# A diffusion block with S5, latent attention and experts: the prologue put in another order

## The chip, the cores and the metric

The kernel runs on one core of a Trainium2 chip. The metric is the device time of one execution in microseconds (us). The engines are TensorE (PE, with its weight loads as PEld), VectorE (DVE), ScalarE (ACT), GpSimd (POOL) and SyncE (SP), which here issues nearly all transfers. Each engine works through its own queue in order.

## The reference, cut to what matters

One layer works on 512 latent tokens and 256 context tokens of width 1024, in float32:

```python
mod_x = silu(c) @ w_ada + b_ada
hx = modulate(rmsnorm(x, norm1_g), sh1x, sc1x)
ux, qax, kvax, krx, gatex = split(hx @ w_in)
lam_bar, b_bar = s5_discretise(lam_re, lam_im, log_dt, b_re, b_im)
xs_x = s5_scan(s5_drive(ux, b_bar), lam_bar, rev, h0)
x_mid = x + g1x * merge_branches(ssm_x, attn_x, gatex, w_out)
x = x_mid + g2x * expert_choice_ffn(hx2, ...)
```

`hc` and `uc` are the same for the context. The change is in the first part: the adaLN shift and scale, the modulated tokens, the input projection and the S5 branch (32 groups of 16 channels, both directions). Attention and the 16 experts follow and are not touched.

## The kernel before, in words

The prologue, up to the end of the input projection, is scheduled by hand: inside `tc.manual_schedule()` every engine runs its instructions in the order in which the program issues them. Buffers come from pools with a fixed count, and an instruction that takes a buffer waits until the former user is done.

The work is this. `pk`, one packed load of small parameters, and the tokens `X` (L215 to L219) are loaded, then the S5 parameters `craw` and `braw` (L220 to L223), then the adaLN weights in four parts (`wada_load`, L227), the last part only after the first half of the tokens has been transposed, since it takes one of their buffers. ScalarE squares the tokens, VectorE normalises them (`xnorm`), TensorE transposes them (`xt_half`, L343) into `xt` for latent and `hc` for context tokens. `rr` deals out the instructions of several generators in turn, which sets VectorE's order; `late_by` delays one of them. Among them are the S5 parameters: `powers` and `powers2` (powers of the discretised eigenvalues: `lt_`, `lq`), `rot` (L429, the rotations `e8`) and `bbar_g` (L453).

The adaLN product (`ada_part`, L188) has eight k-steps of four 32-row matmuls. `ada_end` (L192) copies it to SBUF on ScalarE and turns it into columns `acol`, which give the scale and shift `ab1`. With them the tokens are modulated for each of eight k-tiles: a high part on ScalarE (L636) and a low part on VectorE, two operations (L108 and L93). `mm3` (L120) multiplies in three matmuls: high by high, high by low, low by high.

The input projection has 25 blocks of 128 columns: four `u` (for S5), three `q`, two `kv`, sixteen gate blocks `g`. `win_load` loads a block's weights, `win_prep` (L608) splits them on ScalarE and VectorE into `ws`, a pool of two buffers. `win_block` (L650) does 24 matmuls into a buffer of the pool `psg` (two buffers, by `pg`). `u` and `kv` blocks have a context part too (`ctx_block`, L658), 8 matmuls into another buffer of that pool. `f_kv` (L690) reads its latent product by ScalarE and, for the low part of the result, by VectorE (`stt`).

S5 works in four rounds `gb`. Their parameters come from `s5_P` and `s5_R` on POOL (L507, L571; R needs `e8`), and from `s5_Q` on VectorE (L521), which `s5_B` transposes on TensorE (L531). `s5_K` (L547) makes a kernel of short lags. A round itself is `s5_V` (L755: the drive on TensorE, then multiplications by R, a scan and multiplications again on VectorE), `s5_Y` (L789: output matmuls, which need the scan's result `Xc`), `s5_T` and `s5_out`. Blocks of `fill` (all but the `u` blocks, in the order of `order`) are put between by `fill_one` (L833), so that TensorE has work while VectorE scans: two after each `s5_V`, one after `s5_Y`, one after `s5_out`. The five left over run in a tail, each with one split of weights for the next stage; constants on VectorE (L930 to L970 or so) stand before the tail.

Before the change, block `u` 0 is multiplied alone as tokens are modulated; the other `u` blocks follow, with the parameters of round 0 and 1 between them, and then the rounds.

Of the kernel before, what the change touches and what calls it, by code (L numbers as in the profile page):

```python
# [8 lines left out]
F32 = mybir.dt.float32  # L9
# [46 lines left out]
def hybrid_block(ctx: ExitStack, tc: tile.TileContext, A, out, dbg=None, stop=99):  # L56
# [12 lines left out]
    cur = {}  # L69

    def cst(name, shape, dt=F32, p="const"):
        return (const if p == "const" else cur[p]).tile(shape, dt, name=name, tag=name)

    def tl(p, name, shape, dt=F32):
        return cur[p].tile(shape, dt, name=name, tag=p)
# [139 lines left out]
    for j in range(4):  # L215
# [1 line left out]
        dma(t[0:NCX], cv[:, 2 * j:2 * j + 2, :])  # L217
        dma(t[NCX:NCH], xv[:, 2 * j:2 * j + 2, :])
        X.append(t)  # L219
    craw = cst("craw", [128, 2, 32, 16], p="early")  # L220
    dma(craw, A["ssm_c"])
    braw = tl("qq", "braw", [128, 2, 32, 16])
    dma(braw, A["ssm_b"])  # L223
    hc = tl("hxp", "hc", [128, 8, 256])
    wt = {}

    def wada_load(kh, tags):  # L227
        q = 0
        while q < 4:
            n, big = tags.pop(0)  # L230
            t = tl(n, f"wada{kh}{q}", [128, 2, 2, 512] if big else [128, 1, 2, 512])
            for i in range(1 + big):
                wt[kh, q] = t[:, i]
                dma(t[:, i], wada_src(0, 2, kh, q))
                q += 1

    wada_load(0, [("hxp", 1), ("hxp", 1)])
    wada_load(1, [("hxp", 1), ("hxp", 1)])
    wada_load(2, [("m4", 0), ("m4", 0), ("rr", 0), ("rr", 0)])

    S.activation(sc2v[:, 0], P("c"), AF.Silu)
    S.activation(sc2v[:, 1], P("cc"), AF.Silu)
# [88 lines left out]
    def xnorm(hf):  # L331
        l0 = 4 * hf
        vx = sm("vx", [NCH, 4])
        ts(vx, ssx[:, l0:l0 + 4], 1.0 / D, EPS)
        yield
        yield from rsqrt_g(rstd[:, l0:l0 + 4], vx, [NCH, 4])
        for l in range(l0, l0 + 4):
            ts(X[l // 2][:, l % 2, :], X[l // 2][:, l % 2, :], rstd[:, l:l + 1])
            yield
# [143 lines left out]
    rr(expm1_parts(za, ex, em1), trig(), late_by(5, xnorm(0)))  # L483
    S.activation(sh, br, AF.Sin)
    S.activation(ch, ab, AF.Sin)
    rr(xnorm(1), late_by(2, powers2()), late_by(2, powers()), late_by(8, xt_half(0)))
    wada_load(3, [("zz", 0), ("xc", 0), ("xx", 1)])
    pada = pg("ada0")
    for k in range(2):
        ada_part(pada, k, [wt[0, q][:, k] for q in range(4)])  # L490
    rr(xt_half(1), rot(), late_by(8, bbar_g()))
    for k in range(2, 8):
        ada_part(pada, k, [wt[k // 2, q][:, k % 2] for q in range(4)])

    PTs, RTs, MTs, BTs, Qs = {}, {}, {}, {}, {}
    SH = [128, 8, 8, 16]
# [87 lines left out]

    bd = tl("bd", "bd", [128, 2, 8, 32])
    G.memset(bd, 0.0)
    s5_P(0)
    s5_R(0)
    pha.close()
    for n, k in (("uf", 1), ("sq", 3), ("gt", 3), ("kr", 1), ("ws", 2), ("raw", 4)):  # L590
        cur[n] = pool(n, ph1, bufs=k)
    order = [(f, b) for f, bs in (("u", range(4)), ("g", (0, 1)), ("kv", (0,)), ("g", (2, 3, 4)), ("kv", (1,)),
                                  ("g", (5, 6, 7)), ("q", (0, 1)), ("g", (8, 9)), ("q", (2,)), ("g", range(10, 16)))
             for b in bs]
    base = {"u": 0, "q": 512, "kv": 896, "g": 1184}
    wins, preps = [], {}
    nxt = {"load": 0, "prep": 0}

    def win_load():
        if nxt["load"] < len(order):  # L600
            f, b = order[nxt["load"]]
            nxt["load"] += 1
            w = tl("raw", f"win_{f}{b}", [128, 8, 128])
            c = base[f] + 128 * b
            dma(w, win[:, :, c:c + 128])
            wins.append(w)

    def win_prep():  # L608

        if nxt["prep"] < len(order):  # L610
            fb = order[nxt["prep"]]
            nxt["prep"] += 1
            raw = wins.pop(0)
            ws = tl("ws", "ws", [128, 2, 8, 128], F32R)
            S.activation(ws[:, 0], raw, AF.Copy)
            preps[fb] = ws, raw
            if fb == ("u", 0):
                return
            sub(ws[:, 1], raw, ws[:, 0].bitcast(F32))
            if fb[0] not in ("u", "kv"):  # L620
                win_load()

    for _ in range(4):
        win_load()
    wkr = tl("kr", "wkr", [128, 8, 32])
    dma(wkr, win[:, :, 1152:1184])
    ada_end(0, pada, tl("dt", "adar0", [128, 512]), win_prep)
    ab1 = cst("ab1", [128, 2, 8, 2])
    c0 = acol[:, 0].rearrange("p (u q) b s -> p u (q b) s", u=2)
    V.tensor_copy(ab1[:, 1], c0[:, 0])  # L630
    stt(ab1[:, 0], c0[:, 1], 1.0, P("g1n")[:, :, None].to_broadcast([128, 8, 2]), ALU.add, ALU.mult)
    hx = [[tl("hxp", f"hx{i}{j}", [128, 4, 512], F32R) for j in range(2)] for i in range(2)]
    for k in range(8):
        x = xt[k // 4][:, k % 4, :]
        hi, lo = [hx[i][k // 4][:, k % 4, :] for i in range(2)]
        S.activation(hi, x, AF.Identity, scale=ab1[:, 0, k, 0:1], bias=ab1[:, 1, k, 0:1])  # L636
        S.activation(hc[:, k, :], hc[:, k, :], AF.Identity, scale=ab1[:, 0, k, 1:2], bias=ab1[:, 1, k, 1:2])
        h = tl("gt", "hxf", [128, 512])
        ts(h, x, ab1[:, 0, k, 0:1], ab1[:, 1, k, 0:1])
        sub(lo, h, hi.bitcast(F32))  # L640
        if k == 0:
            ws, raw = preps["u", 0]
            sub(ws[:, 1], raw, ws[:, 0].bitcast(F32))

    def hxs(k, tok=slice(0, 512)):
        return [hx[i][k // 4][:, k % 4, tok] for i in range(2)]

    def win_block(f, b):  # L650

# [3 lines left out]
            mm3(p, [ws[:, i, k, :] for i in range(2)], hxs(k), k == 0, k == 7)  # L655
        return p, raw

    def ctx_block(raw):  # L658
        p = pg("pc", (128, 256))
        for k in range(8):  # L660
            T.matmul(p, raw[:, k, :], hc[:, k, :], start=(k == 0), stop=(k == 7))
        return p
# [175 lines left out]
            later.remove(x)  # L838
            sumsq(*x)

    win_prep()
    s5_Q(0)
    o = f_u(0)
    win_prep()
    u_out(0, *o)
    us_ = {0: s5_U(0)}
    o = f_u(1)
    win_prep()
    u_out(1, *o)
    s5_B(0)  # L850
    o = f_u(2)
    s5_bd(0)
    win_prep()
    u_out(2, *o)
    s5_K(0)
    s5_P(1)
    s5_R(1)
    o = f_u(3)
    win_prep()
    u_out(3, *o)  # L860
    for gb in range(4):
        U, rt = us_.pop(gb)
        Xc = s5_V(gb, U, rt)
        fill_one()
        fill_one()
        win_prep()
        win_prep()
        if gb < 3:
            s5_Q(gb + 1)
        yb = s5_Y(gb, U, Xc)  # L870
        if gb < 3:
            us_[gb + 1] = s5_U(gb + 1)
            s5_bd(gb + 1)
        if gb < 2:
            s5_P(gb + 2)
            s5_R(gb + 2)
        fill_one()
        t, y = s5_T(gb, yb)
        run_late()
        s5_out(gb, t, y)  # L880
        win_prep()
        if gb == 1:
            f_kr()
        fill_one()
        if gb < 3:
            s5_K(gb + 1)
            s5_B(gb + 1)
            win_prep()
# [81 lines left out]
    bh = cst("bh", [128, 4])  # L970
    ts(bh, P("bglu"), 0.5)

    tail = [(), (t_wkv,), (t_wg,), (t_ysp, 0), (t_ysp, 1)]
    while fill:
        win_prep()
        fill_one()
# [660 lines left out]
```

## Time and profile before

| | us |
|---|---|
| median of 3 runs (lowest to highest) | 1933.91 (1933.46 to 1936.47) |
| profiled execution, its own time | 1933.22 |
| its span | 1931.4 |
| TensorE busy in the span | 1661.3 (86%) |
| VectorE busy | 530.1 (27%) |
| ScalarE busy | 320.6 (17%) |
| POOL busy | 209.7 (11%) |
| mean rate of HBM, read and written, over the span | 332 GB/s |

The busy shares are means over stages with different limits. The prologue takes the first 310 us, attention and the router the next 290, the experts the rest. In a timeline line the columns are start, duration, engine, line, operation, output<-inputs, sizes and count, and in brackets the idle time before it and what ended that. The granted clock is 1.00 at TensorE's full 2.4 GHz and 0.50 at 1.2 GHz.

### The profile page before, as it was taken

The page shows a single profiled execution, that of the slowest core. Times are in us where ns is not written, and L with a number is a line of the kernel's source. Part 1 is how long each engine was busy: PE and PEld are TensorE (multiplying, and loading weights), DVE is VectorE, ACT ScalarE, POOL GpSimd, SP SyncE. Part 2 cuts the span into 40 slices and gives each one's busy share as a digit, 9 for nine tenths or more (in the row PEclk, how much of TensorE's full clock was granted, in tenths as well). Part 3 has the DMA queues.
Part 4 walks back from the last instruction along what each step waited for, and adds up shares of the span by engine and source line. Part 5 has one row for each costly group of instructions (what it writes and reads, how often), then busy time and mean ns, then how long its engine had stood idle before and what let it go on. Part 6 is the DMA issues. An engine that isn't in the chain of part 4 may idle for free.

```text
span 1931.4 us, 21472 instructions
## 1 busy us (share of the span) xinstructions
PE 1661.3 (86%) x8660; PEld 806.7 (42%) x8660; DVE 530.1 (27%) x1180; ACT 320.6 (17%) x593; POOL 209.7 (11%) x218
## 2 busy tenths in 40 slices
PE   4798999999996998888888888888888888888887
PEld 2576778755673343323333233333323233332322
DVE  8877655666744100000010010101000010000000
ACT  3422225464421100000000000000000000000000
POOL 3767100231110000000000000000000000000000
PEclk8899999999997999999999999999999999999999
DMA  9253353434675999999999999999999999999997
GB/s 315 64 144 110 109 190 112 169 125 176 170 290 223 419 414 420 414 414 419 414 414 419 414 420 415 419 414 414 420 415 420 414 419 414 414 420 414 420 414 286
DMA packets 149122, 642.61 MB, mean 333 GB/s; under 512 B 14752, under 2 KB 49568, under 8 KB 84128
## 3 DMA queue, kind: packets, MB, share of 16 engines
q1 hardware_dynamic: 145504, 631.81, 82.1%
q0 software_dynamic: 2880, 7.34, 1.7%
q10 hardware_dynamic: 640, 2.10, 0.4%
q8 instruction: 68, 1.11, 0.2%
q14 instruction: 30, 0.25, 0.0%
HBM read 623.93 MB, written 17.27 MB: 332 GB/s over the span
## 4 chain that ended last, share of the span: by engine, by line
PE 45%; DMA 34%; DVE 7%; issue 5%; ACT 3%; POOL 2%; POOLq 0%; SPq 0%; ACTq 0%; DVEq 0%
DMA wu<-in_w_e_up 16%; PE pgu L1504 15%; DMA wg<-in_w_e_gate 9%; DMA wd<-in_w_e_down 8%; PE pdn L1519 8%; PE pxg L1457 2%; PE po L1259 1%; DVE hd L93 1%; PE px L121 1%; PE px L123 1%; PE px L122 1%; ACT hd L1506 1%; PE ada L190 1%; PE phT L1511 1%; PE py L800 1%
## 5 line engine op out<-in xcount | busy, mean ns | idle before, releaser
L1504 PE MATMUL pgu<-wu,xe 128*64 128x512 f32 (+1 forms) x1536 | 630.1, 562 | 31.8 <-DMA wu<-in_w_e_up 31.7
L1504 PE MATMUL pgu<-wg,xe 128*64 128x512 f32 (+1 forms) x1536 | 635.7, 562 | 1.2 <-DVE xe L93 1.2
L1519 PE MATMUL pdn<-wd,hT 128*64 128x512 f32 x1408 | 365.5, 650 | 32.1 <-ACT hT L1513 32.1
L93 DVE TENSOR_TENSOR hd<-hd,pgu 64x512 f32<-64x512 f32 x96 | 62.0, 645 | 1011.4 <-ACT hd L1506 1011.4
L1504 PEld LDWEIGHTS pgu<-wg,xe 128*64 128x64 f32 x1536 | 207.3, 138 | 258.6 <-issue 240.8
L1504 PEld LDWEIGHTS pgu<-wu,xe 128*64 128x64 f32 x1536 | 207.8, 138 | 179.5 <-issue 124.1
L1506 ACT ACTIVATE hd<-pgu 64x512 f32<-64x512 f32 x96 | 53.2, 555 | 967.7 <-PE pgu L1504 967.7
L1519 PEld LDWEIGHTS pdn<-wd,hT 128*64 128x64 f32 x1408 | 114.3, 147 | 215.6 <-issue 164.6
L1538 POOL DMA_INDIRECT out<-ye,sidx x16 | 24.9, 1555 | 1354.9 <-DVE ye L111 1208.4
L1511 PE MATMUL phT<-pk,hd 64*128 64x64 f32 x352 | 42.0, 236 | 118.3 <-DVE hd L93 118.2
L1511 PEld LDWEIGHTS phT<-pk,hd 64*128 64x128 f32 x352 | 28.9, 138 | 195.9 <-DVE hd L93 195.9
L121 PE MATMUL px<-hx,ws 128*128 128x512 f32 x200 | 82.5, 413 | 6.1 <-ACT hx L636 6.1
L122 PE MATMUL px<-hx,ws 128*128 128x512 f32 x200 | 81.0, 405 | 3.3 <-DVE hx L93 3.3
L123 PE MATMUL px<-hx,ws 128*128 128x512 f32 x200 | 80.6, 403 | 1.4 <-DVE ws L93 1.4
L1457 PE MATMUL pxg<-xm,oh 128*64 128x512 f32 x256 | 75.5, 620 | 0.6 <-DVE oh L93 0.6
L1513 ACT COPY hT<-phT 128x256 f32<-128x256 f32 x96 | 34.0, 354 | 119.7 <-PE phT L1511 119.7
L121 PEld LDWEIGHTS px<-hx,ws 128*128 128x128 f32 x200 | 39.1, 195 | 15.3 <-ACT hx L636 6.2
L122 PEld LDWEIGHTS px<-hx,ws 128*128 128x128 f32 x200 | 38.9, 194 | 14.8 <-DVE hx L93 7.5
L123 PEld LDWEIGHTS px<-hx,ws 128*128 128x128 f32 x200 | 38.8, 194 | 10.5 <-DVE ws L93 2.5
L1461 DVE COPY xg<-pxg 128x256 f32<-128x256 f32 x16 | 6.8, 424 | 128.6 <-ACT xg L1460 128.6
L1457 PEld LDWEIGHTS pxg<-xm,oh 128*64 128x64 f32 x256 | 30.1, 142 | 22.9 <-issue 21.3
L1229 DVE TENSOR_REDUCE mx<-ps 128x1 f32<-128x768 f32 x32 | 30.5, 954 | 27.7 <-PE ps L123 25.0
(473 smaller groups left out, 1767.2 us busy)
## 6 DMA issues: line engine op xcount, KB each, us to landing
wg<-in_w_e_gate SPq DMA_DIRECT2D x176, 1024.0 KB, 19.9
wu<-in_w_e_up SPq DMA_DIRECT2D x164, 1024.0 KB, 19.9
wd<-in_w_e_down SPq DMA_DIRECT2D x163, 1024.0 KB, 19.9
wada<-in_w_ada SPq DMA_DIRECT2D x16, 1024.0 KB, 7.3
wd<-in_w_e_down SPq DMA_DIRECT2D x26, 512.0 KB, 18.7
wu<-in_w_e_up SPq DMA_DIRECT2D x24, 512.0 KB, 18.0
wada<-in_w_ada SPq DMA_DIRECT2D x16, 512.0 KB, 10.6
win_g<-in_w_in SPq DMA_DIRECT2D x16, 512.0 KB, 4.2
```

The lines of the kernel that those rows point to most:

```text
L93: (e or V).tensor_tensor(o, a, b, op=op)
L121: T.matmul(o, a[0], b[0], start=first, stop=False)
L122: T.matmul(o, a[0], b[1], start=False, stop=False)
L123: T.matmul(o, a[1], b[0], start=False, stop=last)
L1229: V.tensor_reduce(mx, p[:, 0:768], AX.X, ALU.max, negate=True)
L1457: T.matmul(px[64 * h:64 * h + 64, :], oh[:, t], xms[t][:, 512 * h:512 * h + 512], start=(t == 0), stop=(t == 3))
L1504: T.matmul(p[64 * j:64 * j + 64, :fn], xe[:, k, :], wt_[8 * j + k], start=(k == 0), stop=(k == 7))
L1506: S.activation(hd[:, :fn], p[0:64, :fn], AF.Silu)
L1511: T.transpose(ph[:, b, :], hd[:, 128 * b:128 * b + 128], ident[0:64, 0:64])
L1513: S.copy(hT[:, :n], ph[:, :n])
L1519: T.matmul(po[64 * h:64 * h + 64, :], hT[:, b, :], w[:, 512 * h:512 * h + 512], start=(f0 == 0 and b == 0), stop=(f0 + 128 * b == FF - 128))
L1538: G.indirect_dma_start(out=o2, out_offset=bass.IndirectOffsetOnAxis(ap=sidx, axis=0), in_=ye, in_offset=None, compute_op=ALU.add)
```

## The change

The loads: the fourth part of the adaLN weights goes partly into two buffers of the pool `raw`, which is opened earlier, and so needs no wait for the tokens. The weights of `u` 0 and 1 are loaded next, and only then `craw` and `braw`.

The first 40 us: of the S5 parameters only `powers` and `powers2` stay, beside the second half of the transposes; four adaLN k-steps are dealt between these transposes. `rot` and `bbar_g`, and with them `s5_P(0)` and `s5_R(0)`, move behind the first two blocks. The splits of `u` 0 and `u` 1 are issued ahead of the last four adaLN k-steps and of `ada_end`.

The token loop: for each k-tile both blocks are multiplied (six matmuls). The context modulation moves behind the loop, the two context parts follow, into the other PSUM pool (`pa`).

The rounds: `s5_P(0)`, `s5_R(0)`, `s5_U(0)` come after block 1, `s5_Q(0)` after block 2, `s5_B(0)`, `s5_K(0)` and the parameters of round 1 after block 3. Two gate blocks then run ahead of the first `s5_V`. The number of fill blocks in each round stays the same but for the last, which has one less; the tail has four.

```diff
-    craw = cst("craw", [128, 2, 32, 16], p="early")
-    dma(craw, A["ssm_c"])
-    braw = tl("qq", "braw", [128, 2, 32, 16])
-    dma(braw, A["ssm_b"])
...
     wada_load(2, [("m4", 0), ("m4", 0), ("rr", 0), ("rr", 0)])
+    wada_load(3, [("zz", 0), ("xc", 0), ("raw", 0), ("raw", 0)])
...
+    win_load()
+    win_load()
+    craw = cst("craw", [128, 2, 32, 16], p="early")
+    dma(craw, A["ssm_c"])
+    braw = tl("qq", "braw", [128, 2, 32, 16])
+    dma(braw, A["ssm_b"])
...
-    rr(xnorm(1), late_by(2, powers2()), late_by(2, powers()), late_by(8, xt_half(0)))
-    wada_load(3, [("zz", 0), ("xc", 0), ("xx", 1)])
+    rr(xnorm(1), late_by(8, xt_half(0)))
     pada = pg("ada0")
-    for k in range(2):
-        ada_part(pada, k, [wt[0, q][:, k] for q in range(4)])
-    rr(xt_half(1), rot(), late_by(8, bbar_g()))
-    for k in range(2, 8):
-        ada_part(pada, k, [wt[k // 2, q][:, k % 2] for q in range(4)])
+
+    def ada_first(k0, k1):
+        for k in range(k0, k1):
+            ada_part(pada, k, [wt[k // 2, q][:, k % 2] for q in range(4)])
+            for _ in range(4):
+                yield
+
+    rr(xt_half(1), ada_first(0, 4), late_by(2, powers2()), late_by(2, powers()))
...
-    s5_P(0)
-    s5_R(0)
     pha.close()
...
+    for _ in range(2):
+        win_prep()
+    for k in range(4, 8):
+        ada_part(pada, k, [wt[k // 2, q][:, k % 2] for q in range(4)])
+    ada_end(0, pada, tl("dt", "adar0", [128, 512]))
+    for _ in range(2):
         win_load()
     wkr = tl("kr", "wkr", [128, 8, 32])
     dma(wkr, win[:, :, 1152:1184])
-    ada_end(0, pada, tl("dt", "adar0", [128, 512]), win_prep)
...
+    first = [(pg("px"),) + preps.pop(("u", b)) for b in range(2)]
     for k in range(8):
...
-        S.activation(hc[:, k, :], hc[:, k, :], AF.Identity, scale=ab1[:, 0, k, 1:2], bias=ab1[:, 1, k, 1:2])
...
+        for p, ws, _ in first:
+            mm3(p, [ws[:, i, k, :] for i in range(2)], hxs(k), k == 0, k == 7)
+    for k in range(8):
+        S.activation(hc[:, k, :], hc[:, k, :], AF.Identity, scale=ab1[:, 0, k, 1:2], bias=ab1[:, 1, k, 1:2])
...
-    win_prep()
-    s5_Q(0)
-    o = f_u(0)
-    win_prep()
-    u_out(0, *o)
+    for _ in range(2):
+        win_prep()
+    for b in range(2):
+        pc = ctx_block(first[b][2], pa)
+        win_load()
+        u_out(b, first[b][0], pc)
+    rr(rot(), late_by(8, bbar_g()))
+    s5_P(0)
+    s5_R(0)
     us_ = {0: s5_U(0)}
-    o = f_u(1)
-    win_prep()
-    u_out(1, *o)
-    s5_B(0)
     o = f_u(2)
-    s5_bd(0)
     win_prep()
     u_out(2, *o)
+    s5_bd(0)
+    s5_Q(0)
+    o = f_u(3)
+    win_prep()
+    u_out(3, *o)
+    s5_B(0)
     s5_K(0)
     s5_P(1)
     s5_R(1)
-    o = f_u(3)
-    win_prep()
-    u_out(3, *o)
+    for _ in range(2):
+        fill_one()
+        win_prep()
     for gb in range(4):
         U, rt = us_.pop(gb)
         Xc = s5_V(gb, U, rt)
...
-        win_prep()
+        if gb < 3:
+            win_prep()
         if gb == 1:
             f_kr()
-        fill_one()
         if gb < 3:
+            fill_one()
...
-    tail = [(), (t_wkv,), (t_wg,), (t_ysp, 0), (t_ysp, 1)]
+    tail = [(t_wkv,), (t_wg,), (t_ysp, 0), (t_ysp, 1)]
```

## Rows read from the trace of the kernel before

**Rows 1.** Windows: busy us (x instructions) per engine, granted clock, DMA share, GB/s.

```profile
20.00:40.00 20.00, 11.08 (x68) 6.96 (x72) 19.79 (x47) 3.18 (x7) 14.61 (x10) 0.84 1.06 393
...
60.00:80.00 20.00, 18.03 (x64) 13.07 (x65) 19.29 (x23) 8.09 (x14) 8.05 (x8) 0.81 0.19 54
...
160.00:180.00 20.00, 15.64 (x111) 12.28 (x112) 16.39 (x21) 4.61 (x8) 8.05 (x8) 0.83 0.23 66
...
600.00:1931.00 1331.00, 1129.01 (x5420) 419.17 (x5420) 124.45 (x338) 95.63 (x210) 24.89 (x16) 0.96 0.99 407
```

**Rows 2.** One tile, wada, 0 to 60 us: ns min/median/max, first and last start.

```profile
L234 SPq DMA_DIRECT2D wada<-in_w_ada x16: 367/565/851, 7.7 to 27.6; - x16
...
DMA to landing us min/median/max: 10.1/10.6/11.0
```

**Rows 3.** Timeline, end of adaLN, 35 to 82 us: start us, duration us, engine, line.

```profile
39.86 7.21 PE L190 MATMUL ada<-wada,scv 128*32 128x512 f32 x48
...
40.34 0.19 DVE L93 TENSOR_TENSOR e<-e,nu 128x32 f32<-128x32 f32 x1
...
47.15 0.58 ACT L193 COPY adar<-ada 128x512 f32<-128x512 f32 x1 [6.59 <-PE ada L190]
...
53.49 0.18 DVE L93 TENSOR_TENSOR acol<-adac,pk 128x32 f32<-128x32 f32 x1
...
54.08 0.81 ACT L636 ACTIVATE hx<-xTa,ab 128x512 fp32r<-128x512 f32 x1 [5.39 <-issue]
```

**Rows 4.** Timeline, token loop and second projection block.

```profile
54.03 1.26 DVE L108 TENSOR_SCALAR hxf<-xTa,ab 128x512 f32<-128x512 f32 x1
...
69.08 0.69 DVE L93 TENSOR_TENSOR hx<-hxf,hx 128x512 fp32r<-128x512 f32 x1
...
73.66 0.58 PE L121 MATMUL px<-hx,ws 128*128 128x512 f32 x1
...
79.33 3.62 PE L661 MATMUL pc<-hc,win_u 128*128 128x256 f32 x16
```

**Rows 5.** Timeline of POOL, 60 to 210 us: S5 parameter groups 0 and 1.

```profile
61.76 1.93 POOL L93 TENSOR_TENSOR R<-cm_u,cm_w 128x256 f32<-128x256 f32 x2
...
75.54 2.08 POOL L93 TENSOR_TENSOR PT<-craw,lt 128x1024 f32<-128x1024 f32 x1
...
106.47 1.74 POOL L93 TENSOR_TENSOR R<-cm_u,cm_w 128x256 f32<-128x256 f32 x2
```

**Rows 6.** Timeline of DVE, S5's Q for group 1.

```profile
122.16 1.22 DVE L93 TENSOR_TENSOR Q<-bbar,lq 128x1024 f32<-128x1024 f32 x1
...
125.94 2.96 DVE L93 TENSOR_TENSOR Q<-bbar,lq 128x1024 f32<-128x1024 f32 x1
```

**Rows 7.** Timeline, S5 group 0 from its drive to its output.

```profile
104.28 2.86 PE L766 MATMUL pv<-U,BT 128*64 128x96 f32 x64
...
119.20 0.87 PE L800 MATMUL py<-PT,Xc 64*64 64x128 f32 x12 [0.20 <-DVE Xc L93]
```

**Rows 8.** Timeline of PE, S5 group 1.

```profile
145.50 2.86 PE L766 MATMUL pv<-U,BT 128*64 128x96 f32 x64
...
162.85 0.49 PE L800 MATMUL py<-PT,Xc 64*64 64x128 f32 x4 [3.01 <-DVE Xc L93]
...
164.85 1.54 PE L800 MATMUL py<-PT,Xc 64*64 64x128 f32 x12 [1.51 <-DVE Xc L93]
```

**Rows 9.** Timeline, first kv block's release and the gate block after it.

```profile
135.11 0.74 DVE L111 SCALAR_TENSOR_TENSOR kvo<-px,pk,kvo 128x512 fp32r<-128x512 f32 x1
...
135.90 0.50 PE L121 MATMUL px<-hx,ws 128*128 128x512 f32 x1
```

**Rows 10.** Timeline, last S5 output and the constants before the tail.

```profile
270.39 1.15 PE L811 MATMUL pyT<-pk,yb 64*64 64x64 f32 x32
...
283.20 1.22 DVE L93 TENSOR_TENSOR ws<-win_g,ws 128x1024 fp32r<-128x1024 f32 x1
```

**Rows 11.** Waits of PE, 264 to 325 us: total us, times, longest.

```profile
PE px L123 <- DVE ws L93: 0.5, 1, 0.5
```

More of the change, by code (lines that the diff above doesn't have):

```diff
@@ L204, in wada_src @@
         return wada[:, kn * kh:kn * kh + kn, (4 * t + q) * 512:(4 * t + q + 1) * 512]
+    cur["raw"] = pool("raw", ph1, bufs=4)
     pha = ph1.enter_context(ExitStack())
@@ L239, in hybrid_block, with win_load @@
     wada_load(2, [("m4", 0), ("m4", 0), ("rr", 0), ("rr", 0)])
+    wada_load(3, [("zz", 0), ("xc", 0), ("raw", 0), ("raw", 0)])
+    order = [(f, b) for f, bs in (("u", range(4)), ("g", (0, 1)), ("kv", (0,)), ("g", (2, 3, 4)), ("kv", (1,)),
+                                  ("g", (5, 6, 7)), ("q", (0, 1)), ("g", (8, 9)), ("q", (2,)), ("g", range(10, 16)))
+             for b in bs]
+    base = {"u": 0, "q": 512, "kv": 896, "g": 1184}
+    wins, preps = [], {}
+    nxt = {"load": 0, "prep": 0}
+    def win_load():
+        if nxt["load"] < len(order):
+            f, b = order[nxt["load"]]
+            nxt["load"] += 1
+            w = tl("raw", f"win_{f}{b}", [128, 8, 128])
+            c = base[f] + 128 * b
+            dma(w, win[:, :, c:c + 128])
+            wins.append(w)
+    win_load()
[4 more added lines that the diff above has]
+    dma(braw, A["ssm_b"])
     S.activation(sc2v[:, 0], P("c"), AF.Silu)
@@ L586, in hybrid_block @@
     G.memset(bd, 0.0)
-    s5_P(0)
-    s5_R(0)
     pha.close()
-    for n, k in (("uf", 1), ("sq", 3), ("gt", 3), ("kr", 1), ("ws", 2), ("raw", 4)):
+    for n, k in (("uf", 1), ("sq", 3), ("gt", 3), ("kr", 1), ("ws", 2)):
         cur[n] = pool(n, ph1, bufs=k)
[L592 to L606, printed above, removed]
     def win_prep():
@@ L616, in win_prep @@
             preps[fb] = ws, raw
-            if fb == ("u", 0):
-                return
             sub(ws[:, 1], raw, ws[:, 0].bitcast(F32))
@@ L621, in win_prep @@
                 win_load()
-    for _ in range(4):
+    for _ in range(2):
[4 more added lines that the diff above has]
+    for _ in range(2):
         win_load()
@@ L632, in hybrid_block, with hxs @@
     hx = [[tl("hxp", f"hx{i}{j}", [128, 4, 512], F32R) for j in range(2)] for i in range(2)]
+    def hxs(k, tok=slice(0, 512)):
+        return [hx[i][k // 4][:, k % 4, tok] for i in range(2)]
+    first = [(pg("px"),) + preps.pop(("u", b)) for b in range(2)]
     for k in range(8):
         x = xt[k // 4][:, k % 4, :]
-        hi, lo = [hx[i][k // 4][:, k % 4, :] for i in range(2)]
+        hi, lo = hxs(k)
         S.activation(hi, x, AF.Identity, scale=ab1[:, 0, k, 0:1], bias=ab1[:, 1, k, 0:1])
-        S.activation(hc[:, k, :], hc[:, k, :], AF.Identity, scale=ab1[:, 0, k, 1:2], bias=ab1[:, 1, k, 1:2])
         h = tl("gt", "hxf", [128, 512])
@@ L640, in hybrid_block @@
         sub(lo, h, hi.bitcast(F32))
[L641 to L648, printed above, removed]
+        for p, ws, _ in first:
+            mm3(p, [ws[:, i, k, :] for i in range(2)], hxs(k), k == 0, k == 7)
+    for k in range(8):
+        S.activation(hc[:, k, :], hc[:, k, :], AF.Identity, scale=ab1[:, 0, k, 1:2], bias=ab1[:, 1, k, 1:2])
     def win_block(f, b):
@@ L656, in win_block, with ctx_block @@
         return p, raw
-    def ctx_block(raw):
-        p = pg("pc", (128, 256))
+    def ctx_block(raw, ps=pg):
+        p = ps("pc", (128, 256))
         for k in range(8):
```

## The prediction

> **What bounds the kernel now.** I read the windows first. From 600 us on the DMA share is 0.99 [rows 1]: the expert stage streams weights, and whatever the prologue gains or loses moves that stage by the same amount, because its loads start when buffers come free. So the question lies before 310 us. There TensorE is the bound from about 70 us on, with three kinds of hole: it is busy 11.1 of 20 us at 20 to 40, it runs at a mean granted clock of 0.81 at 60 to 80, and at 160 to 180 it is busy 15.6 of 20 us at 0.83 [rows 1]. Next I read the timeline of the first 80 us. VectorE is busy 19.8 and 19.3 of 20 us in two of these windows [rows 1], much of it on S5 parameters: between the end of the adaLN product (39.86 + 7.21 = 47.1) and the first modulated token tile (54.08) TensorE waits while VectorE finishes them [rows 3]. Last I read, for each S5 group, what its output matmuls wait for, and the waits of the tail. The span of the profiled execution is 1931.4 us, its time 1933.2, the median of the runs 1933.9; I sum against 1933.2.
>
> **Step 1, tokens and adaLN first.** The last adaLN weight is issued at 27.6 and lands 10.6 later, at 38.2 [rows 2]. The two S5 loads of 0.52 MB each go behind it: 1.05 MB at 393 GB/s [rows 1] is 2.7 us, so it lands at 35.5. Two of the eight adaLN steps are then left, 2.4 us by 7.21 us for six [rows 3]: 37.9. ScalarE now has two weight copies ahead of the adaLN copy. Their weights land behind adaLN's, 1.3 us each, so the copy ends near 39.8 and not 38.5. The small adaLN matmuls and three short VectorE operations follow. Before, the 13 us of S5 work from 40.34 to 53.49 [rows 3] stood in their way; now only two weight splits do. Modulated tokens start near 42.3, instead of 54.08.
>
> **Step 2, two blocks side by side.** Per k-tile VectorE makes one low part. The loop of eight tiles took from 54.03 to 69.77 [rows 4]; three tiles and a weight split, which the change moves ahead, stood before POOL's end at 63.7 [rows 5], some 2.5 us a tile, and five in the 6.1 us after it, 1.25 a tile. Now POOL's first S5 part (which waits for its late load, 39.6) lies beside the loop until about 56: five tiles at 2.5 and three at 1.25 end near 58.6. TensorE needs 5.67 us for 24 matmuls of a block [rows 4], 1.4 us per tile for both blocks, and ends near 60.5. Before, the second block, its context part aside, would have ended at 79.3 - 3.5 = 75.8. **Gain 15.3 us.** Bounds: 10.5 if the clock stays at its lower level through the loop, 17 if the first POOL part disturbs it less.
>
> **Step 3, what is late next: S5's Q.** Behind the loop TensorE has two context parts (3.5 us each), then blocks 2 and 3 with theirs (9.2 each): until 85.9. Then it needs Q of group 0, from VectorE. VectorE must first split the weights of blocks 2 and 3, and these wait in its queue until the loop has released their buffers (2.5 us, to 63), with the whole S5 chain behind them. That chain took 13.1 us [rows 3]; I take 12.5, to 75.5, and one split to 77. POOL's R of group 0 needs that chain; it ended 10.2 us behind it before (63.7 against 53.5) [rows 3, 5], so now at 86, and the second group's P and R, 32.7 us [rows 5], end at 118.5. Q therefore runs beside POOL throughout. Its first half took 3.8 us with POOL idle (122.16 to 125.94), the second half 9.2 with POOL busy, until 135.11 [rows 6, 9]. Two halves at 8 give 93. Before, the same Q was covered by a slower TensorE. The last transposes of Q thus start some 4.5 us late, and the clock falls: **6.5 us lost** with 2 for the clock, the price read from group 1, where 12 output matmuls after a wait took 1.54 us instead of 0.87 [rows 7, 8]. Bounds: 0 if Q is done by 86, and 9.5.
>
> The Trainium skill (SBUF — State Buffer, section Who interferes with whom) says that a VectorE instruction with two SBUF inputs and a GpSimd instruction that reads SBUF exclude each other for the whole instruction. The doubled second half of Q agrees in kind; an estimate by that rule, with at least 1 us of POOL ahead of each of Q's ten operations (7.6 us by themselves), makes Q 17.6 us or more instead of 16, and the loss 8 or more.
>
> **Step 4, S5 two blocks later.** Two gate blocks (11.3 us) now stand ahead of group 0's drive, which starts at 104.3 + 11.3 - 8.8 = 106.8. They were its cover. Behind the drive there now come the first kv block and a gate block. The kv block takes both buffers of its PSUM pool, and one is read by a VectorE operation. VectorE works in order, and that operation stands behind the whole scan chain. In the trace this dependency is seen at the later place: the gate block started at 135.90, when that read ended at 135.85 [rows 9]. The output could go on 14.9 us after the drive's start in group 0, with POOL idle, and 19.3 in group 1, with POOL busy [rows 7, 8]. With R of group 1 until 118.5, I take 17.5, plus 0.75 for the read: 18.3. TensorE has 2.86 + 5.67 + 3.5 = 12.0 us of work, then waits 6.3 where it waited 0.2 [rows 7]. With the clock, **8.4 lost**; bounds 3.5 and 10. In group 1 the same happens with the second kv block: POOL's next group starts when group 0's output frees its buffer, and the drive now comes some 5 us closer behind that output. The two waits there were 4.5 us together [rows 8] and become 9: **4.5 lost**, bounds -1 and 6. Groups 2 and 3 have small matmuls as extra cover: 1 gained.
>
> **Step 5, the tail.** Between the last S5 output and the tail VectorE computes constants; the split of the next weights came at 283.20, 12.8 us after the last S5 transposes started (270.39) [rows 10]. Two prepared gate blocks covered it, and the wait was 0.5 us [rows 11]. Now one is left there: 1.1 + 5.67 us of cover against 10.4 + 1.2 (one split and one sum of squares less ahead of it), and two matmuls that need no low part. 4 us of wait and 2 of clock: **6 lost**, bounds 2 and 7.
>
> Costed at nothing: the moved weight loads (the queue has space behind adaLN, and blocks 2 and 3 need theirs only at 67; if they were late, TensorE would wait up to 4 us there); ScalarE's context modulation behind the loop (six spare us in it); the second PSUM pool for the first context parts, unused then.
>
> **Sum.** -15.3 + 6.5 + 8.4 + 4.5 - 1 + 6 = +9.1: 1942.3, said as 1942.
>
> **Rivals.** *The lead stays* (faster). If VectorE, no longer between adaLN and the tokens, keeps ahead, Q is in time and the drive's chain runs at its 14.9 us. For it: the change removes no work, and VectorE has idle stretches later. Then -15.3, +3.5 at the first kv block, nothing in group 1, 3 in the tail: -8.8, so 1924.5. It decides at one point: Q of group 0 done by 86 us. *A wash*: the front end comes only 10.5 sooner and the new waits take just that, or the S5 chain through POOL and VectorE sets the pace of the whole prologue whatever TensorE does; 1934. The reordering would then not do what it says. *The clock stays low in the token loop* (slower still): the window of the loop before had 0.81 [rows 1], and TensorE worked there in short pieces; twice the pieces may not lift it. At half the clock 48 matmuls of 0.47 us from 42.8 end at 65.3, 4.8 later: 1947. *A longer Q*: both halves at 9.2 and the split ahead slowed too, 3.4 more, 1946; for it, the operations of one shape that took 1.22 and 2.96 us [rows 6]. The rule named in step 3 would give at least half of this.
>
> **How the numbers follow.** Forecast 0.40, low clock 0.12, longer Q 0.10: slower 0.62. Lead stays 0.24, wash 0.14. What a measurement of this kernel can tell from no change is about 0.2%, 4 us. The slower cases alone span 1936 to 1953; with half of the faster case the range is 1926 to 1953.
>
> **What would show it.** First modulated tile near 42 us and both blocks done near 60; a wait of TensorE on Q's transposes near 90; one of 5 us or more ahead of the gate block behind the first kv block, released by VectorE's read of the kv block; a longer one in group 1; one for a weight split in the tail. If the first two hold and the waits are missing, the lead stays and I am wrong. If the tokens start later than 46, step 1 is wrong.

## The result and the profile after

The changed kernel takes 1953.87 us (median of 5 runs, 1947.46 to 1956.5), the kernel before 1933.46 in the same runs: ratio 1.0101, interval 1.0080 to 1.0122. So the reordering costs 1%, some 20 us. The forecast was 1942; the direction was right, the loss was twice as large. The profiled execution after is the slowest of the five (time 1956.5, span 1954.7), 2.6 above the median.

First the windows of the kernel after (busy us and instructions of PE, PEld, DVE, ACT, POOL; granted clock; DMA share; GB/s):

```profile
20.00:40.00 20.00, 18.60 (x116) 10.21 (x116) 14.60 (x68) 6.09 (x13) 0.00 (x0) 1.00 1.06 395
...
60.00:80.00 20.00, 18.82 (x83) 15.61 (x84) 16.99 (x60) 4.99 (x9) 4.76 (x10) 1.00 0.32 96
...
120.00:140.00 20.00, 12.18 (x60) 9.84 (x57) 17.65 (x25) 1.93 (x4) 10.89 (x10) 0.80 0.30 93
...
180.00:200.00 20.00, 9.44 (x34) 7.34 (x32) 12.19 (x12) 1.33 (x3) 10.36 (x8) 0.74 0.19 66
```

The early windows became what the change is after: 18.6 of 20 us at 20 to 40 where it was 11.1, and the full clock at 60 to 80 where it was 0.81 [rows 1]. But two new holes stand at 120 to 140 and at 180 to 200. The waits of PE from 0 to 340 us say whose they are (total us, times, longest):

```profile
PE px L121 <- DVE kvo L111: 18.4, 2, 10.6
PE pbt L561 <- DVE Q L93: 6.8, 2, 4.9
PE px L123 <- DVE ws L93: 4.4, 1, 4.4
PE pkrt L745 <- DVE kr L741: 3.8, 1, 3.8
...
PE py L810 <- DVE Xc L93: 1.1, 2, 0.6
```

The first three are the ones that the prediction named: the kv blocks' buffer held for VectorE's read, S5's Q, the split in the tail (0.5 before [rows 11]). Their places in PE's timeline:

```profile
41.13 1.90 PE L190 MATMUL ada<-wada,scv 128*32 128x512 f32 x10 [0.20 <-DMA wada<-in_w_ada]
...
49.26 0.79 PE L121 MATMUL px<-hx,ws 128*128 128x512 f32 x1 [2.52 <-ACT hx L649]
...
68.20 7.07 PE L671 MATMUL pc<-hc,win_u 128*128 128x256 f32 x32
...
92.92 0.60 PE L561 MATMUL pbt<-pk,Q 128*128 128x128 f32 x4
...
98.42 1.97 PE L561 MATMUL pbt<-pk,Q 128*128 128x128 f32 x8 [4.90 <-DVE Q L93]
...
117.71 2.86 PE L776 MATMUL pv<-U,BT 128*64 128x96 f32 x64
...
137.51 0.80 PE L121 MATMUL px<-hx,ws 128*128 128x512 f32 x1 [7.82 <-DVE kvo L111]
...
169.38 2.86 PE L776 MATMUL pv<-U,BT 128*64 128x96 f32 x64
...
191.93 0.80 PE L121 MATMUL px<-hx,ws 128*128 128x512 f32 x1 [10.56 <-DVE kvo L111]
...
235.51 2.86 PE L776 MATMUL pv<-U,BT 128*64 128x96 f32 x64
...
312.07 0.50 PE L123 MATMUL px<-hx,ws 128*128 128x512 f32 x1 [4.36 <-DVE ws L93]
```

The last adaLN steps waited for their weights until 41.13, the first product of modulated tokens came at 49.26, both blocks were done when their context parts began at 68.20, the first drive came at 117.71 where it was 104.28 [rows 7]. VectorE's timeline shows why the buffer was held:

```profile
54.00 2.15 DVE L108 TENSOR_SCALAR hxf<-xTa,ab 128x512 f32<-128x512 f32 x1
...
62.71 0.54 DVE L108 TENSOR_SCALAR hxf<-xTb,ab 128x512 f32<-128x512 f32 x1
...
71.14 0.18 DVE L93 TENSOR_TENSOR nu<-cb 128x32 f32<-128x32 f32 x1
...
72.78 0.19 DVE L93 TENSOR_TENSOR e<-e,nu 128x32 f32<-128x32 f32 x1
...
86.86 2.07 DVE L93 TENSOR_TENSOR Q<-bbar,lq 128x1024 f32<-128x1024 f32 x1
...
100.73 1.43 DVE L93 TENSOR_TENSOR Q<-Q,qu 128x512 f32<-128x512 f32 x1
...
121.00 0.55 DVE L93 TENSOR_TENSOR zb__1157<-pv,R 128x384 f32<-128x384 f32 x1
121.58 1.32 DVE L93 TENSOR_TENSOR z<-za__1156,zb__1157 128x384 f32<-128x384 f32 x1
...
128.41 4.41 DVE L787 TENSOR_TENSOR_SCAN z<-rt,z 128x768 f32<-128x768 f32 x2
...
136.72 0.74 DVE L111 SCALAR_TENSOR_TENSOR kvo<-px,pk,kvo 128x512 fp32r<-128x512 f32 x1
```

The read of the kv block at 136.72 is the next thing that VectorE does after the whole scan chain; 0.05 after its end the gate block starts. The wait also costs clock: the eleven matmuls from 137.51 to 142.38 follow each other at 0.44 us, the later ones at 0.23. The same lines show what POOL does to VectorE: an operation of one shape takes 2.15 us at 54 and 0.54 at 62.71, once POOL's first part has ended (61.58).

### The profile page after: what moved, and what is told of

It is laid out like the page before. It is cut to its first block, busy times and chain, and to the rows that moved or that the text cites. A ratio compares the mean times of both kernels' runs of the same rounds, so it can differ in the third digit from the quotient of the medians.

```text
span 1954.7 us, 21485 instructions
## 1 busy us (share of the span) xinstructions
PE 1665.9 (85%) x8660; PEld 811.7 (42%) x8660; DVE 534.2 (27%) x1180; ACT 320.9 (16%) x593; POOL 216.6 (11%) x218
## 4 chain that ended last, share of the span: by engine, by line
DMA 38%; PE 25%; issue 4%; DVE 2%; ACT 2%; POOLq 0%; SPq 0%; ACTq 0%; DVEq 0%
DMA wu<-in_w_e_up 18%; PE pgu L1520 12%; DMA wg<-in_w_e_gate 11%; DMA wd<-in_w_e_down 9%; PE pdn L1535 6%; PE pxg L1473 2%; DVE hd L93 1%; ACT hd L1522 1%; PE phT L1527 1%; PE pxm L123 1%; PE pxm L122 1%; PE pxm L121 1%; DMA out<-ye,sidx 0%; PE pxt L1480 0%; ACT hT L1529 0%
## 5 line engine op out<-in xcount | busy, mean ns | idle before, releaser
L1535 PE MATMUL pdn<-wd,hT 128*64 128x512 f32 x1408 | 363.6, 647 | 32.4 <-ACT hT L1529 32.4
L121 PE MATMUL px<-hx,ws 128*128 128x512 f32 x200 | 85.6, 428 | 20.9 <-DVE kvo L111 18.4
L122 PE MATMUL px<-hx,ws 128*128 128x512 f32 x200 | 83.2, 416 | 3.6 <-DVE hx L93 3.6
L123 PE MATMUL px<-hx,ws 128*128 128x512 f32 x200 | 82.2, 411 | 4.4 <-DVE ws L93 4.4
L121 PEld LDWEIGHTS px<-hx,ws 128*128 128x128 f32 x200 | 40.5, 202 | 31.9 <-DVE kvo L111 19.2
L122 PEld LDWEIGHTS px<-hx,ws 128*128 128x128 f32 x200 | 40.5, 202 | 14.5 <-DVE hx L93 6.4
L123 PEld LDWEIGHTS px<-hx,ws 128*128 128x128 f32 x200 | 40.4, 202 | 13.6 <-DVE ws L93 4.8
## 6 DMA issues: line engine op xcount, KB each, us to landing
wu<-in_w_e_up SPq DMA_DIRECT2D x24, 512.0 KB, 18.2
```

Source lines behind the costliest of these rows:

```text
L121: T.matmul(o, a[0], b[0], start=first, stop=False)
L122: T.matmul(o, a[0], b[1], start=False, stop=False)
L123: T.matmul(o, a[1], b[0], start=False, stop=last)
L1535: T.matmul(po[64 * h:64 * h + 64, :], hT[:, b, :], w[:, 512 * h:512 * h + 512], start=(f0 == 0 and b == 0), stop=(f0 + 128 * b == FF - 128))
```

## A second profile of the kernel before, and the loss stage by stage

**f0: the kernel before, unchanged.** The tokens after landed up to 13.2 us after their issue, in the first profile of before up to 8.9. Is that the change?

> The kernel before, unchanged, for a second profile of it. If the landing of the tokens varies from execution to execution by itself, they land anywhere from 8.9 to 13 us after their issue here too, and the start of the token loop (54.03 in the first profile) moves little, since VectorE's S5 work stands ahead of it. If the kernel before loads them more quickly by its order of loads, they land within 9 us again. Time within 0.2% of 1933.

It took 1933.91 us. In this second profile the tile view of the token buffer says of its eight loads:

```profile
DMA to landing us min/median/max: 4.2/9.6/12.7
```

and the timeline of PE has the first product of modulated tokens and the first three drives at:

```profile
58.95 0.80 PE L121 MATMUL px<-hx,ws 128*128 128x512 f32 x1 [5.52 <-ACT hx L636]
...
108.28 2.86 PE L766 MATMUL pv<-U,BT 128*64 128x96 f32 x64
...
149.55 2.86 PE L766 MATMUL pv<-U,BT 128*64 128x96 f32 x64
...
206.39 2.86 PE L766 MATMUL pv<-U,BT 128*64 128x96 f32 x64
```

So the unchanged kernel's loads vary too, and its prologue moves with them: the tokens start 4.0 later than in the first profile (54.94), the first drive 4.0 later, the last S5 transposes 3.65 later (274.04). My expectation that the loop would move little was wrong. The prediction had been worked out from an execution with quick loads. Like is to be compared with like: this profile (tokens 12.7) with the one after (13.2). The table gives after minus f0, less the 11.3 us of two gate blocks from the first drive to the last S5 transposes, since after has done two more by then.

| point in the program | predicted | f0 to after | lost or gained since the line above |
|---|---|---|---|
| first modulated tile | -11.8 | -9.7 | -9.7 |
| blocks u 0 and u 1 done | -15.3 | -11.5 | -1.8 |
| first drive (V of group 0) | -8.8 | -1.9 | +9.6 |
| second drive | -0.4 | +8.5 | +10.4 |
| third drive | +4.1 | +17.8 | +9.3 |
| last S5 transposes | +3.1 | +15.1 | -2.7 |
| projection done, next stage's first product | +9.1 | +20.0 | +4.9 |
| span | +9.1 | +22.6 | +2.6 |

("u 1 done" in f0 is the start of its second context part, 83.33, less the first, 3.6.) One line is less firm than the others: from the second drive to the third the unchanged program took 58.3 us in the first profile, 56.8 here and 54.8 in f1 below, which has the same S5 rounds, with nearly the same waits but a granted clock of 0.88, 0.91 and 0.94; after took 66.1. What the prologue lost reached the end whole (22.6 us in this pair, 20.4 by the medians), as the first paragraph of the prediction had it.

## The experiments

The kernel before was timed beside each; the ratios are to it.

| kernel | median us (lowest to highest), runs | ratio to before (95%) |
|---|---|---|
| e1 the changed kernel again | 1952.63 (1949.02 to 1954.12), 4 | 1.0106 (1.0091 to 1.0121) |
| e2 kv blocks back in third place | 1938.01 (1935.92 to 1942.85), 5 | 1.0040 (1.0026 to 1.0053) |
| e3 tail: split ahead of the constants | 1949.66 (1948.88 to 1951.61), 4 | 1.0100 (1.0085 to 1.0115) |
| e4 gate blocks ahead of Q's transposes | 1953.11 (1950.54 to 1955.26), 4 | 1.0111 (1.0095 to 1.0126) |
| f1 before, S5 loads later | 1933.52 (1931.76 to 1936.76), 10 | 1.0011 (1.0000 to 1.0022) |
| f2 changed, S5 loads first | 1954.21 (1951.61 to 1955.94), 4 | 1.0115 (1.0097 to 1.0133) |
| e6 = e2 + e3 | 1931.64 (1928.36 to 1938.22), 12 | 1.0001 (0.9989 to 1.0014) |
| e5 = e2 + e3 + e4 | 1931.82 (1930.20 to 1933.35), 12 | 0.9993 (0.9984 to 1.0003) |
| g7 = e6, S5 parameters early | 1930.81 (1928.37 to 1935.80), 12 | 0.9999 (0.9988 to 1.0010) |
| g8 changed, kv read from a copy | 1935.63 (1931.71 to 1940.59), 12 | 1.0023 (1.0012 to 1.0033) |
| h1 = e6, part of POOL's work left out | 1924.04 (1922.66 to 1926.42), 6 | 0.9960 (0.9946 to 0.9973) |

**e1: the changed kernel once more**, with a second profile.

> The changed kernel once more. Its token loads landed up to 13.2 us after their issue, against 8.9 in the kernel before, at some 235 GB/s against 310. If that comes from the new order of the program (addresses, or what is queued behind the tokens), the last token load again lands near 18 us and the first modulated tile starts near 48 us; if it was chance of one execution, it lands near 14 us and the first tile starts near 44 us. Time 1954, give or take 4.

The same waits (18.6 for the kv read, 6.9 for Q, 4.4 in the tail), with tokens that landed within 12.3 us.

**e2: the kv blocks back in third place.** Two gate blocks go ahead of the first kv block again.

```diff
-    ("g", (0, 1)), ("kv", (0,)), ("g", (2, 3, 4)), ("kv", (1,)), ("g", (5, 6, 7)), ("q", (0, 1)), ...
+    ("g", (0, 1, 2, 3)), ("kv", (0,)), ("g", (4, 5, 6)), ("kv", (1,)), ("g", (7,)), ("q", (0, 1)), ...
```

> The changed kernel with each kv block back in third place of its S5 round, behind the output matmuls, and a gate block in its stead behind the drive. Theory of the waits: the 18.4 us that TensorE waited for VectorE's read of the kv blocks go, 0.5 to 5 us of waits on the scan's result come in their place, and the clock no longer falls in round 0: 12 to 15 us faster than the changed kernel, near 1941. Rival, that the S5 chain through POOL and VectorE sets the pace: the drive of the next round comes no sooner, the time stays between 1950 and 1956.

Waits of PE of this kernel:

```profile
PE py L810 <- DVE Xc L93: 8.6, 6, 3.0
PE pbt L561 <- DVE Q L93: 6.9, 2, 4.9
```

The 18.4 us are gone; waits for the scan come in their place, 8.6 where it had 1.1. The order of the fill blocks alone is worth 14.6 us against e1 by the medians, two thirds of the 21.6 us that e1 loses to the kernel before in the same runs.

**g8: the same wait taken away in another way.** The order stays as changed; ScalarE copies the kv product to SBUF and VectorE's low part reads the copy, so the buffer no longer waits for VectorE.

```diff
+        xs = tl("gt", "kvx", [128, 512])
+        S.copy(xs, p)
...
-            stt(o[1][:, c], x, g, o[0][:, c].bitcast(F32), ALU.mult, ALU.subtract)
+            stt(o[1][:, c], xs if x is p else x, g, o[0][:, c].bitcast(F32), ALU.mult, ALU.subtract)
```

> The changed kernel, with one thing more: ScalarE copies the latent product of a kv block to SBUF, and VectorE's low part reads that copy, so that the PSUM buffer no longer waits for VectorE. Theory (the buffer held for VectorE's read behind the scan is what the early kv blocks cost): the 18.4 us of waits for that read go, waits for the scan's result of 1 to 9 us come in their place, and the time is near 1940, some 12 to 14 lower than the changed kernel, as with the kv blocks put back. Rival (the chain of drive and scan sets the pace, and the read was only where TensorE happened to stop): the same wait stands one block later ahead of the output matmuls, and the time stays at 1950 or above.

Waits of PE of this kernel:

```profile
PE px L121 <- ACT kvo L712: 3.1, 2, 1.5
...
PE py L812 <- DVE Xc L93: 1.9, 3, 1.0
```

By the ratios to the kernel before (1.0023, against 1.0101 and 1.0106 of the changed kernel) this is some 15 to 16 us less, a little more than forecast. Two different edits take the wait away and both get most of the loss back: it is the buffer held behind the scan, not the scan itself, that cost it.

**e3: the tail.** The first split of the tail is issued ahead of the constants; the later ones move by one.

> The changed kernel with the first weight split of the tail issued ahead of the constants, not behind them. Theory of the waits: the 4.4 us wait of TensorE on that split goes, and 1 us or 2 of lower clock with it: 5 to 6 us faster than the changed kernel, near 1948.5. Rival: the attention's first tiles, which need these constants and splits, come no sooner, the time stays at 1954.

The wait for `ws` is gone. The medians differ by 3.0 us from e1, less than expected, and the two intervals overlap, so that alone this gain is not shown; with the kv order right (e2 to e6) it is 6.4, and those intervals lie apart.

**e4: two gate blocks ahead of Q's transposes**, so that TensorE has work while Q is finished:

```diff
-    s5_B(0)
-    s5_K(0)
...
+    s5_B(0)
+    s5_K(0)
```

(the two lines move behind the two gate blocks that run ahead of the first drive)

> The changed kernel with the two early gate blocks ahead of the transposes of Q and the lag kernel of group 0, not behind them. Theory of the waits: Q is done when its transposes are reached, the 6.8 us of wait and 2 us of lower clock go, the drive of group 0 starts some 9 us sooner; of this up to 3 us come back as a longer wait for the kv block's read, since POOL is still busy: 6 to 9 us faster than the changed kernel, near 1946. Rival, that POOL and VectorE set the pace: the read of the kv block ends at the same time as in the changed kernel (137 to 138 us) and the time stays between 1951 and 1956.

Waits of PE of this kernel:

```profile
PE px L121 <- DVE kvo L111: 19.2, 2, 10.5
PE px L123 <- DVE ws L93: 7.6, 2, 4.4
...
PE px L121 <- ACT uf L682: 2.0, 1, 2.0
```

Q's wait is gone and the time is the same, as the rival had it. The gate blocks need a weight split, which is queued on VectorE behind Q: of the 6.8 us, 3.2 come back as waits for a split, 2.0 for `uf` and 0.8 for the kv block's read; the wait has mostly another name. e5, with the same edit on e6, says it again:

> All three edits together: kv blocks third, first tail split ahead of the constants, gate blocks ahead of the transposes of Q. Theory of the waits: with no kv read behind the drive the sooner drive counts now, so 15 + 3.5 + 4 to 7 off the changed kernel: 1927 to 1931, no slower than the kernel before. Rival, that POOL and VectorE set the pace of the S5 rounds: the third edit again gives nothing: 1934 to 1936.

> Two of the edits: kv blocks third and the first tail split ahead of the constants. If their gains add up (15 and 3.5): 1934 to 1935. What is then left against the kernel before is the wait for Q's transposes (6.9 us) against the head start.

With the kv order and the tail mended (e6), the changed kernel cannot be told from the kernel before, 2 to 3 us better than expected; e5 is no better, where 4 to 7 us were expected. In e6 the tokens come 9.4 us earlier than in the first profile of before (45.52 and 54.94, loads of 9.8 and 8.9), the two blocks are done 11.3 earlier (64.45), but the first drive, less two gate blocks, only 2.2 (113.40 - 11.3 and 104.28), and nothing is left at the next stage's first product (311.96 and 311.54). So the whole head start is eaten again.

**f1 and f2: which loads stand beside the tokens.** f1 is the kernel before with `craw` and `braw` behind three parts of the adaLN weights; f2 is the changed kernel with them directly behind the tokens.

> The kernel before with nothing changed but the two S5 loads, which go behind three parts of the adaLN weights instead of behind the tokens. If the tokens load slower because of what is queued right behind them (adaLN weights in 2 KB pieces instead of S5 rows of 4 KB), the last token load lands near 18 us instead of 14, as in the changed kernel. If it is something else of the changed kernel (its buffers' addresses), it lands near 14. Time: the S5 chain on VectorE still stands between adaLN and the tokens, so 1931 to 1937.

> The changed kernel with the two S5 loads back behind the tokens and ahead of adaLN. If the neighbour in the queue slowed the tokens, they land near 14 us again, the adaLN weights land no later than in the changed kernel (1.05 MB more ahead of them, 4.6 us sooner begun), and POOL's first S5 part starts near 38 instead of 45 us, so that the loop's end and the S5 chain come 2 to 4 us sooner: 1949 to 1953. If it was the addresses, the tokens land near 18 and the time is 1953 to 1957.

The tokens landed within 10.4 and 11.6 us, neither at 13 nor at 9. With one execution each, against a swing of 3.8 us in one and the same program, a share of the neighbours in the queue cannot be told. Neither kernel's time moved from its own order's by more than can be told. f1's timeline of PE holds a lesson of its own:

```profile
42.58 1.06 PE L198 MATMUL adac<-pk,adar 128*128 128x8 f32 x8 [0.68 <-ACT adar L193]
59.45 0.79 PE L121 MATMUL px<-hx,ws 128*128 128x512 f32 x1 [15.82 <-ACT hx L636]
```

adaLN is done 10 us sooner than in f0 (whose same product stood at 52.37; in the first profile it was 47.78), and the tokens start where they did: VectorE is busy with S5 work without a gap from 32.4 to 58.5. The late start of the tokens in the kernel before was VectorE's, as the prediction read [rows 3]; an earlier adaLN alone is worth nothing here. (The S5 loads are later in f1, so that POOL's P lies beside that work until 47 and stretches part of it.)

**g7: the S5 parameters early, where VectorE has time.** On e6, the rotations and half of `bbar` are dealt into the second half of the transposes, POOL gets R and P of group 0 before the token loop, and Q goes ahead of a split.

```diff
-    rr(xt_half(1), ada_first(0, 4), late_by(2, powers2()), late_by(2, powers()))
+    rr(xt_half(1), ada_first(0, 4), late_by(2, powers2()), late_by(2, powers()),
+       late_by(8, rot()), late_by(12, take(bb, 9)))
...
+    s5_R(0)
+    s5_P(0)
     (token loop)
...
-    rr(rot(), late_by(8, bbar_g()))
-    s5_P(0)
-    s5_R(0)
+    rr(bb)
...
+    s5_Q(0)
```

> The kernel with kv blocks in third place and the split tail (1931.64), with the rotations and the first nine operations of bbar dealt into the second half of the transposes, R and P of group 0 issued on POOL just before the token loop, and Q of group 0 ahead of the split of block 2. Theory (what is left of the head start is eaten because VectorE's own queue of rotations, bbar and Q, the last beside POOL, sets when the first drive can start): Q is done near 90, no wait for its transposes, the first drive near 105 where that kernel has 113.4, and the time near 1923, 8 to 9 lower than that kernel and below the kernel before. Rival (the pace is set elsewhere, by the chain of drive and scan or by the weight splits on VectorE): a weight split or the tokens take Q's place, the first drive comes at 110 or later, and the time is 1929 to 1933.

The theory fell as I had put it. Q was in time (its wait is gone), but POOL now worked beside the whole token loop: the loop took 23.5 us instead of 18.9. It also began 5.3 later (50.78), half of that because adaLN's weights came later in this execution, and ended at 74.30 instead of 64.45; the first drive came at 118.43 instead of 113.40. Yet the time is the same, because the second drive came 42.2 us after the first, not 47.5: POOL was now quiet beside the scan. POOL's work moved, and what it costs VectorE moved with it. f2 has the reverse: POOL's first part starts 8 us sooner there (37.15), and the loop takes 15.4 us.

**h1: less work for POOL.** This kernel leaves out 8 of the 10 POOL operations of P for two of the groups, so it does not compute the layer; it tests directly whether POOL's work is on the path.

```diff
-        for d in range(2):
+        for d in range(2 if gb > 1 else 0):
             u = tl("ptmp", "pu", [128, 4, 8, 16])
             (a product and a sum on POOL; the same in the second loop of s5_P)
```

> The kernel with kv blocks in third place and the split tail (1931.64), with 8 of the 10 POOL operations of P left out for groups 0 and 1 (the products with the imaginary part; P then holds half of its sums), some 11 us of POOL each time; nothing is changed on the other engines. Theory (what is left of the head start goes into VectorE's operations that run beside POOL's: token loop, Q, and above all the scan chain of group 0, which ran beside R of group 1 and took 16.2 us where it took 13.5 with POOL idle): the token loop ends some 3 earlier, POOL is done before the first scan, the waits for the scan's result in round 0 (2.9 and 1.3) go, the stretch from the first drive to the second is 42 to 43 us where it was 47.5, and the time is 1921 to 1925, below both kernels. Rival (POOL's work is off the path; the low clock, the weight splits or the loads take the rest): the stretch stays at 46 or more and the time within 0.2% of 1931.6.

Token loop and round 0 in e6, from PE's timeline (first product, end of the loop, first drive, output, second drive):

```profile
45.52 0.80 PE L121 MATMUL px<-hx,ws 128*128 128x512 f32 x1 [1.70 <-ACT hx L649]
...
64.45 7.07 PE L671 MATMUL pc<-hc,win_u 128*128 128x256 f32 x32
...
113.40 2.86 PE L776 MATMUL pv<-U,BT 128*64 128x96 f32 x64
...
130.68 0.69 PE L810 MATMUL py<-PT,Xc 64*64 64x128 f32 x4 [2.94 <-DVE Xc L93]
...
134.78 1.97 PE L810 MATMUL py<-PT,Xc 64*64 64x128 f32 x16
...
160.88 2.86 PE L776 MATMUL pv<-U,BT 128*64 128x96 f32 x64
```

The wait for the scan's result is 2.94 us where it was 0.20 [rows 7]. The scan on VectorE:

```profile
124.54 4.44 DVE L787 TENSOR_TENSOR_SCAN z<-rt,z 128x768 f32<-128x768 f32 x2
```

The same on PE in h1:

```profile
47.66 0.79 PE L121 MATMUL px<-hx,ws 128*128 128x512 f32 x1 [2.01 <-ACT hx L649]
...
62.84 7.07 PE L671 MATMUL pc<-hc,win_u 128*128 128x256 f32 x32
...
112.56 2.86 PE L776 MATMUL pv<-U,BT 128*64 128x96 f32 x64
...
126.83 0.44 PE L810 MATMUL py<-PT,Xc 64*64 64x128 f32 x4
...
129.76 1.09 PE L810 MATMUL py<-PT,Xc 64*64 64x128 f32 x16
...
154.72 2.86 PE L776 MATMUL pv<-U,BT 128*64 128x96 f32 x64
```

and its scan on VectorE:

```profile
121.49 3.40 DVE L787 TENSOR_TENSOR_SCAN z<-rt,z 128x768 f32<-128x768 f32 x2
```

It held, with one miss: the token loop takes 15.2 us from its first matmul instead of 18.9, the scan 3.40 instead of 4.44, the 2.94 us wait is gone (one of 1.33 stays) and with it the low clock behind it (16 output matmuls in 1.09 us, not 1.97); from drive to drive it is 42.2 us, not 47.5. The kernel is 0.4% faster than before, 0.9960 (0.9946 to 0.9973), with nothing changed on TensorE or VectorE themselves. The gain lies in the loop (3.7 us) and between the drives (5.3). Between the loop's end and the first drive nothing was gained (49.7 us, 49.0 in e6): R of group 0, which was not cut, still lies beside Q, and Q's waits are 7.6 us instead of 6.8. That VectorE is slowed, and does not just wait for results of POOL that come late, is read from the durations of its operations; in e6 neither VectorE nor TensorE has a wait for POOL between 60 and 200 us. Of the versions that do all the work none beats the kernel before.

One run is missing: the kernel before with the same work left out. In that kernel, too, POOL lies beside VectorE (the scan of group 1 takes 5.06 us for the 3.40 of group 0), so it might gain as much. That POOL's work is on the path of the new order is shown; that the head start would count if POOL had less to do is not.

## Why the prediction was off, step by step

**The steps that failed are sizes, in two places.** The first is the pair of terms for the head start and for what it gives back (steps 1 to 3): -15.3 and +6.5 in the sum, -11.5 and +9.6 by the table, so 6.9 of the 13.5 us between +9.1 and the +22.6 of the profiled pair. The second is round 1 of step 4: +4.5 in the sum, +9.3 by the table, 4.8 more. Round 0 and what follows the prologue add 2.0 and 2.6; rounds 2 and 3 and the tail take 1.7 and 1.1 off. The mechanism was the one named: each wait that was forecast came, at its place, and one more (for `kr`, in round 1). Part of the 22.6 is chance: the profiled execution after lies 2.6 us above its median.

- *Step 1.* adaLN's weights were to land at 35.5; the last was awaited until 41.13. The forecast took the landing of one execution (38.2 [rows 2]) and moved it by 2.7; in the second profile the same kernel issues that load at 32.1, not 27.6, because its tokens came later. But e6, with the same early part as after and tokens within 9.8 us, still waited until 37.38: some 2 us of the 5.6 are the forecast's own. From there to the first matmul on the tokens it was 8.1 us (49.26 - 41.13), forecast 6.8 to the first tile (42.3 - 35.5), which lies 0.9 ahead of its matmul: this part was right.
- *Step 2.* The loop was forecast at 18.2 us from the first modulated tile and took 18.9 from its first matmul, 0.9 behind that tile. POOL did lie beside it, until 61.6, and five tiles were slow, as forecast.
- *Step 3.* The rotations and `bbar` took VectorE 14.7 us, from 71.14 to 85.8, not 12.5. The forecast had read this chain from 40.34 on, but in the kernel before it begins earlier, among the copies of the transposes:

```profile
32.56 1.07 DVE L93 TENSOR_TENSOR nu<-cb 128x32 f32<-128x32 f32 x1
```

  So the first nine operations were left out; after the change they take 1.6 us (71.14 to 72.78), and the rest takes 13.0, much as before. Q then took 15.3 us (86.86 to 102.16), forecast 16. Its two waits were 6.8 us, forecast 4.5; the rest of the 9.6 stands in no wait (the granted clock was 0.79 at 100 to 120, 1.00 in f0). The value lies at the upper bound, 9.5; the one taken was too low. My reading that one wait is the price was too narrow: e4 took the wait away and gained nothing, because VectorE's splits for the gate blocks stand behind Q.
- *Step 4, round 0:* +8.4 forecast, +10.4. The chain was to run 18.3 us from the drive to the end of the read; it ran 19.8 (117.71 to 137.46), since the scan itself stretches beside POOL (4.41 us; 3.40 in h1 with POOL idle).
- *Step 4, round 1:* +4.5 forecast, outside its bound of 6 at +9.3 (7.8 against the first profile's stretch, 11.3 against f1's). Three things came on top of the forecast: the single wait is 10.6 us, where I had both waits of [rows 8] at 4.5 become 9; the wait for `kr`, which stood in no term, grew from 1.4 to 3.8; some 0.9 stands in no wait.
- *Rounds 2 and 3:* -1 forecast, -2.7. *Step 5, the tail:* +6 forecast, +4.9; e3 and e6, where the wait is gone, show the mechanism.

Of the rivals, *the lead stays* was wrong at its own point: Q was done at 102, not by 86. *The clock stays low in the token loop* was wrong: 1.00 at 60 to 80. The *wash* was named as the S5 chain through POOL and VectorE setting the pace whatever TensorE does. It is what remains when the two avoidable losses are mended: e6, e5 and g7 are all within 0.1% of before, and h1 shows that POOL's work is part of the chain. The forecast treated it as an alternative to the new waits, but the two add up: the chain eats the head start, and the waits come on top.

The Trainium skill (SBUF — State Buffer, section Who interferes with whom) says that a VectorE instruction contends with a GpSimd instruction that reads SBUF when both its inputs are in SBUF, and that one with at most one SBUF input does not, outside the two-port modes. The trace agrees on both halves: beside POOL's R, `zb<-pv,R`, with one input in PSUM, took 0.55 us, and `z<-za,zb` of the same size 1.32, where with POOL idle (h1) it took 0.56. The `hxf` operation above, with one tensor input in SBUF, stretched even so, 2.15 us against 0.54; in which mode it ran no run here shows. By the estimate from that page in the prediction Q would have been 17.6 us or more; 15.3 were measured, nearer to the rows' 16.

## What to carry to other kernels

In this kernel, work taken off the critical engine's start was worth only what the engine that feeds it could follow. So before moving a step, list all that the feeding engine still has to do before the next dependent point, and which neighbour slows it while it does. When an order shifts by two blocks, look at which block holds a shared buffer until an in-order engine is through with a long chain; it should be one with cover behind it. And take a second profile of the unchanged kernel before trusting a difference of a few microseconds at its start.

## What the hardware showed that I had not expected

The same first loads landed within 8.9 (before) to 13.2 us (after, e4) in the fourteen profiled executions, all of which issue them first; 8.9 and 12.7 are the same program, and so are 12.3 and 13.2. What decides it stays open. And moving POOL's work did not lessen its cost to VectorE here: P and R of a group, 15 us or more each, slow down VectorE's operations beside them, in the token loop (g7), in Q (after) or in the scan (e6).
